# Gate and value written to HBM separately, and multiplied when the down projection loads them

## The chip, the cores and the metric

The kernel runs on one core of a Trainium2 chip. The metric is the device time of one execution in microseconds (us), lower is better. The engines are PE (matrix products; PEld is its weight load), DVE (vector), ACT (activation), POOL (GpSimd; here it mostly issues DMAs) and SP (it only issues DMAs). They run side by side, each in its own fixed order, and wait for one another by semaphores. The order on each engine is set when the kernel is built.

## What is computed

One decoder layer over 512 positions and 2048 channels: a token mixer of four parallel groups, an output projection, and a channel mixer. Only the channel mixer is touched:

```
def conv_ffn(h, up, conv_w, conv_b, down):
    hid = causal_dwconv(h @ up, conv_w, conv_b)      # 2 x 5632 channels, width 3
    gate, val = jnp.split(hid, 2, axis=-1)
    return (jax.nn.gelu(gate) * val) @ down          # 5632 -> 2048
```

All data are float32. A product of two float32 matrices is made of three products of split operands: each operand is a high part (rounded by a cast on ACT, L159 or L1047) and a low part (operand minus high part, a subtraction on DVE, L160 or L1048), and `mul3` (L207 to L211) adds high x high (L209), low x high and high x low (L210, L211).

## The kernel before

The 5632 hidden channels are 44 blocks of 128 channels x 512 positions; f counts them. For each f the **up phase** makes the gate block and the value block. For f from 3 to 43 `up_pair` (L1003) does this with seven smaller products instead of eight, in this order: p1 (B11), p5 (T1), p6 (T2), p2 (B21), p7 (T3), p4 (T4), p3 (B22), each of 24 matmuls over 256 columns. One pass over f is called a pair below; there are 41 of them.

Each pair loads four weight pieces of 512 KB through SP: r11, r21, r22, r12. They go round three buffers `raw`, so a load waits until DVE and ACT have read what the buffer held. DVE forms sums of them (`s1` = r21 + r22, then `s2`, and r21 + r11 in place) and the low parts (`wlo`), ACT the high parts (`whi`). r12 takes the buffer that r11 leaves; the r22 of the next pair takes the buffer that this pair's r22 leaves. Then `gated` (L935) runs the convolution on both blocks (ACT L327, then two steps of DVE L329 for each of gate `fcg` and value `fcv`), the gelu on ACT (L939), the product on DVE (L942), and POOL writes the block to HBM as `gd[f]` (L943).

The **down phase** loads the 44 blocks back, 22 in each half h. `load_g` (L1038) puts a block into a part of `act_hi`/`act_lo` that the up phase no longer reads, or into a buffer `gb`, and splits it. `GAT` (L1034) names the part: blocks 0 to 7 get parts that come free while the last pair runs, 12 to 15 those that its product p4 reads, 8 to 11 those that its p3 reads. PE then multiplies blocks and down weights into banks `pd`, 12 matmuls of 512 columns for one block. The weights are loaded by SP and split like those of the up phase; `whi` and `wlo` have four buffers each.

POOL issues its DMAs in one order: what stands behind a DMA that waits, waits too. The tiles with tag t (`fg`, `fv`, `fcg`, `fcv`, later the four rows of the post-norm) share eight buffers. The scheduler that sets the order simulates the program; so a change in one place can move instructions elsewhere.

Of the kernel before, what the change touches and what calls it, by code (L numbers as in the profile page):

```python
# [7 lines left out]
F32 = mybir.dt.float32  # L8
# [3 lines left out]
ALU = mybir.AluOpType  # L12
# [3 lines left out]
P = 128  # L16
S = 512
# [6 lines left out]
NF = DFF // P  # L24
# [32 lines left out]
def trunk(ctx: ExitStack, tc: tile.TileContext, x, xT, cols, rows, gdn_row, sgu_row, w_in, w_ba,  # L57
          lru_wa, lru_wx, sgu_ws, w_out, ffn_up, ffn_down, out):
    nc = tc.nc
    v, a, g, pe = nc.vector, nc.scalar, nc.gpsimd, nc.tensor  # L60
# [7 lines left out]
    dr = ctx.enter_context(tc.tile_pool(name="dr", bufs=1, space=DRAM))  # L68
# [9 lines left out]
    def new(tag, name, dt=F32):  # L78
        return tp.tile([P, S], dt, tag=tag, name=name, bufs=NBUF[tag])

    def T(name):
        return new("t", name)
# [34 lines left out]
    def col(name, i=0):  # L117
        o, _ = _OFF[name]
        return colt[:, o + i:o + i + 1]
# [141 lines left out]
    for c in range(DC):  # L261
        raw = []
# [58 lines left out]
    def conv(dst, src, taps, bias=None):  # L321

        n = len(taps)
        if bias is None:
            a.activation(out=dst, in_=src, func=AF.Copy, scale=taps[-1])
        else:
            a.activation(out=dst, in_=src, func=AF.Identity, scale=taps[-1], bias=bias)  # L327
        for j in range(1, n):
            v.scalar_tensor_tensor(out=dst[:, j:], in0=src[:, :S - j], scalar=taps[n - 1 - j], in1=dst[:, j:],  # L329
                                   op0=ALU.mult, op1=ALU.add)  # L330
# [62 lines left out]
    for t in range(NTT):  # L393
# [21 lines left out]
                    in1=gcum.rearrange("p t h -> p (t h)"), op=ALU.subtract)  # L415
# [407 lines left out]
    def B(name, dt=F32):  # L823
        return tp.tile([P, 2 * S], dt, tag="b", name=name, bufs=18)

    def side(t, i):
        return t[:, i * S:(i + 1) * S]
# [59 lines left out]
    for t in range(NTT):  # L887
# [22 lines left out]
        for d in range(DC):  # L910
# [3 lines left out]
            if d % 2 == 0:  # L914
# [4 lines left out]
                            in1=colt[:, o + 4 * d:o + 4 * d + 4].rearrange("p (k o) -> p k o", o=1)  # L919
# [2 lines left out]
            a.copy(out=hh, in_=blk(h1))  # L922
            v.tensor_tensor(out=hl, in0=blk(h1), in1=hh.bitcast(F32), op=ALU.subtract)  # L923

    gd = [dr.tile([P, S], F32, name=f"gd{f}") for f in range(NF)]
    o_cv = _OFF["ffn_conv"][0] + 3 * NF
    ncv = tp.tile([P, 3 * NF], F32, tag="ncv", name="ncv", bufs=1)
    v.tensor_scalar_mul(ncv, colt[:, o_cv:o_cv + 3 * NF], -1.0)
# [1 line left out]
    def taps(f, minus=False):  # L930
        if minus:
            return [ncv[:, 3 * (f - NF) + i:3 * (f - NF) + i + 1] for i in range(3)]
        return [col("ffn_conv", 3 * f + i) for i in range(3)]

    def gated(f, gs, vs, minus):  # L935

        gt = T("fcg")
        conv(gt, gs, taps(f), bias=col("ffn_cb", f))
        a.activation(out=gt, in_=gt, func=AF.Gelu_apprx_tanh)  # L939
        vt = T("fcv")  # L940
        conv(vt, vs, taps(NF + f, minus), bias=col("ffn_cb", NF + f))
        v.tensor_tensor(out=vt, in0=vt, in1=gt, op=ALU.mult)  # L942
        nc.gpsimd.dma_start(out=gd[f], in_=vt)  # L943

    NPL = 3
    for f in range(2):
        gemm_half(1, *first[f])
    gated(0, first[0][0], first[1][0], False)


# [20 lines left out]
    for f in range(1, NPL):  # L971
        pg, pv = (gemm_T(ffn_up, ff * P) for ff in (f, NF + f))
        gated(f, pg, pv, False)
# [29 lines left out]
    def up_pair(f):  # L1003
        r11, r21, r22, r12 = (load(ffn_up, k0, 8, ff * P, P) for ff, k0 in
                              ((f, 0), (NF + f, 0), (NF + f, 8), (f, 8)))
        s1, s2 = B("s1"), B("s2")
        gs, vs = T("fg"), T("fv")
        g1, g2, v1, v2 = gs[:, 0:H2], gs[:, H2:], vs[:, 0:H2], vs[:, H2:]
        add(s1, r21, r22)
        p1 = product(split(r11), "B11")  # L1010
        a.copy(out=v1, in_=p1)
        add(s2, s1, r11)
        p5 = product(split(s1), "T1")
        add(r21, r21, r11)
        p6 = product(split(s2), "T2")
        add(g2, v1, p6)
        p2 = product(split(r12), "B21")
        add(g1, v1, p2)
        add(s2, s2, r12)
        p7 = product(split(r21), "T3")  # L1020
        add(v1, g2, p7)
        add(v2, v1, p5)
        add(g2, g2, p5)
        p4 = product(split(r22), "T4")
        add(v1, v1, p4)
        p3 = product(split(s2), "B22")
        add(g2, g2, p3)
        gated(f, gs, vs, True)
# [9 lines left out]
    def load_g(f, i):  # L1038
        if i < 16:
            t, k = GAT[i]  # L1040
            hi, lo = (u[:, t, 4 * k:4 * k + 4, :].rearrange("p k c -> p (k c)") for u in (act_hi, act_lo))
        else:
            b = B("gb", F32R)
            hi, lo = side(b, 0), side(b, 1)
        raw = lo.bitcast(F32)
        nc.gpsimd.dma_start(out=raw, in_=gd[f])
        a.copy(out=hi, in_=raw)  # L1047
        v.tensor_tensor(out=lo, in0=raw, in1=hi.bitcast(F32), op=ALU.subtract)  # L1048
        return hi, lo

    fb = [[B("facc") for _ in range(2)] for _ in range(NTT)]
# [33 lines left out]
    for h in range(2):  # L1085
        gs = []
        for c in range(DC):
            banks = [bank("pd") for _ in range(NTT)]
            by_k = NH // 2 if h == 0 or c < DC - 1 else 7
            for i in range(by_k):  # L1090
                if c == 0:
                    gs += [load_g(h * NH + 2 * i + n, 2 * i + n) for n in range(2)]
                wt = weights(h, i, c)
                for n in range(2):
                    k = 2 * i + n
                    for t in range(NTT):
                        mul3(banks[t], cut(gs[k], TS[t]), wt[n], k == 0, k == NH - 1)
            if h == 1 and c == DC - 1:
                x1r = []
                for t in range(NTT):  # L1100
                    x1r.append((act_hi, act_lo)[t % 2][:, t // 2].rearrange("p k c -> p (k c)").bitcast(F32))
                    nc.sync.dma_start(out=x1r[t], in_=x1d[TS[t], :])
                wts = [weights(h, i, c) for i in range(by_k, NH // 2)]
            for t in range(NTT):
                if h == 1 and c == DC - 1:
                    for i, wt in enumerate(wts):
                        for n in range(2):
                            k = 2 * (by_k + i) + n
                            mul3(banks[t], cut(gs[k], TS[t]), wt[n], False, k == NH - 1)
                if h == 0:  # L1110
                    a.copy(out=facc[t][c], in_=banks[t])
                    continue
                v.tensor_tensor(out=facc[t][c], in0=banks[t], in1=facc[t][c], op=ALU.add)
                finish(t, c)
# [62 lines left out]
```

## Time and profile before

| | |
|---|---|
| time of three runs | 2188.92, 2192.87, 2194.44 us (median 2192.87) |
| the profiled execution | 2188.41 us, its span 2186.7 us |
| PE busy | 2150.3 us (98%), 13146 matmuls |
| DVE busy | 1389.4 us (64%) |
| ACT busy | 895.5 us (41%) |
| POOL busy | 133.5 us (6%) |
| up phase, pairs alone | about 855 to 1689 us from the span's start |
| down phase | about 1689 us to the end |
| gd written | 44 DMAs of 256 KB, median 4.4 us from issue to landing |
| gd loaded | 44 DMAs of 256 KB, medians 4.0 us (32 into act_lo) and 4.9 us (12 into gb) |

The busy share of an engine is an average; which wait ends last in a stage is what sets its time. A busy PE has matmuls that overlap (each is shown 0.28 us long, while they start every 0.12 us), so a short stall of PE is seen in the starts of its matmuls rather than as idle time.

### The profile page before, as it was taken

To read this page: it belongs to the slowest core of one execution; us is meant where nothing else is said; L and a number is where in the kernel's file an instruction comes from. 1 tells how busy PE (TensorE), PEld (TensorE's weight loads), DVE (VectorE), ACT (ScalarE), POOL (GpSimd) and SP (SyncE) were. 2 spreads that over 40 slices of the span, in tenths; PEclk is the share of its full clock that TensorE was granted. 3 is DMA by queue.
4 is the path that set the end of the run, shared out by engine and by line. 5 is a ranking of instruction groups with operands and counts; after the bars stand their busy time and mean duration, and the time that the engine had idled before them with its cause. 6 is when DMAs were issued, how large, how long until landed. Compare 5 with 4: busy or idle time off the path is not lost.

```text
span 2186.7 us, 32062 instructions
## 1 busy us (share of the span) xinstructions
PE 2150.3 (98%) x13146; PEld 1922.1 (88%) x13146; DVE 1389.4 (64%) x1869; ACT 895.5 (41%) x1255; POOL 133.5 (6%) x192
## 2 busy tenths in 40 slices
PE   8999999999999999999999999999999999999997
PEld 7788888888878888999999999999999888888885
DVE  6774454844552496888899999898889322423333
ACT  6564252522432473434444444444445312422222
POOL 0001010101100110000000000000002000100002
PEclk9999999999999999999999999999999999999998
DMA  9233222323232443334344434433436522532233
GB/s 299 68 88 87 68 78 78 78 77 87 87 123 102 155 131 103 115 111 120 105 124 121 119 115 124 122 116 112 122 116 206 179 97 97 166 114 97 96 114 147
DMA packets 316691, 254.85 MB, mean 117 GB/s; under 512 B 10496, under 2 KB 265216, under 8 KB 316032
## 3 DMA queue, kind: packets, MB, share of 16 engines
q1 hardware_dynamic: 304768, 219.24, 33.5%
q0 software_dynamic: 8320, 27.27, 3.4%
q10 hardware_dynamic: 3456, 6.29, 0.9%
q8 instruction: 103, 1.69, 0.3%
q14 instruction: 44, 0.36, 0.0%
HBM read 232.85 MB, written 19.92 MB: 116 GB/s over the span
## 4 chain that ended last, share of the span: by engine, by line
PE 72%; issue 14%; DVE 6%; DMA 6%; ACT 1%; POOL 1%; DVEq 0%; SPq 0%; ACTq 0%; POOLq 0%
PE pT L211 12%; PE pT L210 12%; PE pT L209 12%; DMA raw<-in_ffn_up_dram 5%; PE pd L209 4%; PE pB L211 4%; PE pd L210 4%; PE pB L210 4%; PE pB L209 4%; PE pd L211 4%; PE pwo L211 2%; PE pwo L209 2%; PE pwo L210 2%; DVE wlo L160 2%; DVE s L1001 1%
## 5 line engine op out<-in xcount | busy, mean ns | idle before, releaser
L160 DVE TENSOR_TENSOR wlo<-raw,whi 128x1024 fp32r<-128x1024 f32 x378 | 463.7, 1227 | 449.1 <-ACT whi L159 447.5
L159 ACT CAST whi<-raw 128x1024 fp32r<-128x1024 f32 x378 | 396.1, 1048 | 766.6 <-PE pd L211 295.3
L210 PE MATMUL pT<-act_lo,whi 128*128 128x512 f32 (+1 forms) x1032 | 365.0, 354 | 2.7 <-DVE act_lo L923 2.7
L209 PE MATMUL pT<-act_hi,whi 128*128 128x512 f32 (+1 forms) x1032 | 364.7, 354 | 0.4 <-ACT act_hi L922 0.4
L211 PE MATMUL pT<-act_hi,wlo 128*128 128x512 f32 (+1 forms) x1032 | 364.5, 353 | 0.0
L211 PE MATMUL pT<-eh,wlo 128*128 128x256 f32 x984 | 278.1, 283 | 5.0 <-DVE wlo L160 4.8
L211 PE MATMUL pB<-act_hi,wlo 128*128 128x256 f32 x984 | 278.9, 283 | 0.5 <-DVE wlo L160 0.3
L209 PE MATMUL pB<-act_hi,whi 128*128 128x256 f32 x984 | 278.4, 283 | 0.0
L210 PE MATMUL pB<-act_lo,whi 128*128 128x256 f32 x984 | 278.3, 283 | 0.0
L209 PE MATMUL pT<-eh,whi 128*128 128x256 f32 x984 | 277.1, 282 | 0.0
L210 PE MATMUL pT<-el,whi 128*128 128x256 f32 x984 | 277.0, 282 | 0.0
L159 ACT CAST whi<-s 128x1024 fp32r<-128x1024 f32 x123 | 128.5, 1044 | 231.6 <-DVE s L1001 176.6
L210 PEld LDWEIGHTS pT<-act_lo,whi 128*128 128x128 f32 x1032 | 195.9, 190 | 27.8 <-DVE act_lo L923 2.9
L211 PEld LDWEIGHTS pT<-act_hi,wlo 128*128 128x128 f32 x1032 | 196.0, 190 | 24.9 <-issue 1.0
L209 PEld LDWEIGHTS pT<-act_hi,whi 128*128 128x128 f32 x1032 | 195.8, 190 | 25.0 <-issue 0.7
L209 PE MATMUL pd<-whi,act_hi 128*128 128x512 f32 x512 | 198.5, 389 | 1.0 <-ACT whi L159 1.0
L211 PE MATMUL pd<-whi,act_lo 128*128 128x512 f32 x512 | 199.4, 389 | 0.0
L210 PE MATMUL pd<-wlo,act_hi 128*128 128x512 f32 x512 | 199.3, 389 | 0.0
L211 PEld LDWEIGHTS pT<-eh,wlo 128*128 128x128 f32 x984 | 185.2, 188 | 7.2 <-DVE wlo L160 7.2
L211 PEld LDWEIGHTS pB<-act_hi,wlo 128*128 128x128 f32 x984 | 188.6, 192 | 1.5 <-DVE wlo L160 1.5
L209 PEld LDWEIGHTS pB<-act_hi,whi 128*128 128x128 f32 x984 | 188.7, 192 | 0.2
L210 PEld LDWEIGHTS pB<-act_lo,whi 128*128 128x128 f32 x984 | 188.6, 192 | 0.0
(370 smaller groups left out, 3518.5 us busy)
## 6 DMA issues: line engine op xcount, KB each, us to landing
raw<-in_ffn_up_dram SPq DMA_DIRECT2D x176, 512.0 KB, 4.1
raw<-in_ffn_down_dram SPq DMA_DIRECT2D x88, 512.0 KB, 3.7
raw<-in_w_in_dram SPq DMA_DIRECT2D x86, 512.0 KB, 3.9
raw<-in_w_out_dram SPq DMA_DIRECT2D x32, 512.0 KB, 3.9
gd<-fcv POOLq DMA_DIRECT2D x44, 256.0 KB, 4.4
act_lo<-gd POOLq DMA_DIRECT2D x32, 256.0 KB, 4.0
xs<-in_xT_dram SPq DMA_DIRECT2D x16, 256.0 KB, 6.3
xn<-in_x_dram SPq DMA_DIRECT2D x16, 256.0 KB, 6.1
```

The lines of the kernel that those rows point to most:

```text
L159: a.copy(out=hi, in_=r)
L160: v.tensor_tensor(out=lo, in0=r, in1=hi.bitcast(F32), op=ALU.subtract)
L209: pe.matmul(p, lhsT=lt[0], rhs=rt[0], start=first, stop=False)
L210: pe.matmul(p, lhsT=lt[0], rhs=rt[1], start=False, stop=False)
L211: pe.matmul(p, lhsT=lt[1], rhs=rt[0], start=False, stop=last)
L1001: v.tensor_tensor(out=o, in0=x, in1=y, op=ALU.add)
```

## The change

The product on DVE (L942) goes out of `gated`. Gate and value are written to HBM as two blocks, `gd[f]` and `vd[f]`. In the down phase `load_g` loads both, the value into a new tile `vr` of tag t, multiplies them on DVE, and splits the product.

```
-    gd = [dr.tile([P, S], F32, name=f"gd{f}") for f in range(NF)]
+    gd, vd = ([dr.tile([P, S], F32, name=f"{n}{f}") for f in range(NF)] for n in ("gd", "vd"))
...
-        v.tensor_tensor(out=vt, in0=vt, in1=gt, op=ALU.mult)
-        nc.gpsimd.dma_start(out=gd[f], in_=vt)
+        nc.gpsimd.dma_start(out=gd[f], in_=gt)
+        nc.gpsimd.dma_start(out=vd[f], in_=vt)
...
         raw = lo.bitcast(F32)
         nc.gpsimd.dma_start(out=raw, in_=gd[f])
-        a.copy(out=hi, in_=raw)
-        v.tensor_tensor(out=lo, in0=raw, in1=hi.bitcast(F32), op=ALU.subtract)
+        vr = T("vr")
+        nc.gpsimd.dma_start(out=vr, in_=vd[f])
+        v.tensor_tensor(out=vr, in0=raw, in1=vr, op=ALU.mult)
+        a.copy(out=hi, in_=vr)
+        v.tensor_tensor(out=lo, in0=vr, in1=hi.bitcast(F32), op=ALU.subtract)
```

In the changed kernel the writes are L942 (gd) and L943 (vd), the load of the value L1048, the product L1049, the cast L1050 and the subtraction L1051. The instructions move at three places.

DVE at the start of the sixth pair (f = 8). `wlo<-raw` is the low part of r11, `s<-raw` is s1, `raw<-raw` frees r11. Before:

```order
L942 TENSOR_TENSOR fcv<-fcv,fcg 128x512
L1001 TENSOR_TENSOR fg<-fv,pT_7726 128x256
L160 TENSOR_TENSOR wlo<-s_7657,whi 128x1024
L1001 TENSOR_TENSOR fg<-fv,pB_7756 128x256
L1001 TENSOR_TENSOR s_7894<-raw 128x1024
L160 TENSOR_TENSOR wlo<-raw,whi 128x1024
L1001 TENSOR_TENSOR s_7895<-s_7894,raw 128x1024
L1001 TENSOR_TENSOR raw<-raw 128x1024
```

and now:

```order
L1001 TENSOR_TENSOR fg<-fv,pT_7770 128x256
L160 TENSOR_TENSOR wlo<-s_7701,whi 128x1024
L1001 TENSOR_TENSOR fg<-fv,pB_7800 128x256
L160 TENSOR_TENSOR wlo<-raw,whi 128x1024
L1001 TENSOR_TENSOR s_7938<-raw 128x1024
L1001 TENSOR_TENSOR fv<-fg,pT_7831 128x256
L1001 TENSOR_TENSOR s_7939<-s_7938,raw 128x1024
L1001 TENSOR_TENSOR raw<-raw 128x1024
```

The low part of r11 now stands ahead of s1. Before, it stands behind s1 in the first nine pairs and ahead of it from the tenth on; now it stands behind it in the first five only.

POOL at the end of the up phase, from the DMAs that wait for the last pair's p3 on. Before:

```order
L1046 DMA act_lo_91<-gd8_6233 128x512
L1046 DMA act_lo_91<-gd10_6235 128x512
L1046 DMA act_lo_91<-gd9_6234 128x512
L1046 DMA act_lo_91<-gd11_6236 128x512
L943 DMA gd42_6267<-fcv_16210 128x512
L943 DMA gd43_6268<-fcv_16448 128x512
```

and now:

```order
L1046 DMA act_lo_91<-gd9_6234 128x512
L1046 DMA act_lo_91<-gd11_6236 128x512
L1048 DMA vr_16513<-vd0_6269 128x512
L1048 DMA vr_16519<-vd1_6270 128x512
L1048 DMA vr_16555<-vd2_6271 128x512
L1048 DMA vr_16561<-vd3_6272 128x512
L1048 DMA vr_16597<-vd4_6273 128x512
L943 DMA vd43_6312<-fcv_16492 128x512
L942 DMA gd43_6268<-fcg_16487 128x512
L1048 DMA vr_16603<-vd5_6274 128x512
```

All value loads, that of block 0 first, stand behind the loads of blocks 9 and 11, which wait for the last up product.

ACT at the same place. `fcg` and `fcv` are the last pair's convolution, L939 its gelu, `whi` weights. Before:

```order
L1047 CAST act_hi<-act_lo 128x512 x3
L159 CAST whi<-raw 128x1024
L327 ACTIVATE fcg<-fg,colt 128x512
L327 ACTIVATE fcv<-fv,colt,ncv 128x512
L831 DMA row<-in_rows_dram 128x512 x4
L159 CAST whi<-raw 128x1024
L939 ACTIVATE fcg<-fcg 128x512
```

and now:

```order
L159 CAST whi<-raw 128x1024 x4
L327 ACTIVATE fcg<-fg,colt 128x512
L327 ACTIVATE fcv<-fv,colt,ncv 128x512
L939 ACTIVATE fcg<-fcg 128x512
L1050 CAST act_hi<-vr 128x512 x8
L159 CAST whi<-raw 128x1024
```

The last pair's convolution and gelu come ahead of the first cast of a loaded block, where they stood behind nearly all of them. On PE, the three down matmuls that stood inside the last pair's p3 now stand behind it.

## Rows read from the trace of the kernel before

**Rows 1.** Stretches: length, busy PE, PEld, DVE, ACT, POOL; granted clock, DMA share, GB/s.
```profile
860.00:1106.00 246.00, 241.66 (x2000) 239.26 (x2000) 211.07 (x266) 107.47 (x126) 6.27 (x12) 1.00 0.39 113
1106.00:1600.00 494.00, 494.00 (x4139) 493.99 (x4138) 450.10 (x569) 230.86 (x273) 13.49 (x25) 1.00 0.41 120
```
**Rows 2.** What PE waited for, whole span: us in total, times, longest us.
```profile
PE pT L211 <- DVE wlo L160: 4.8, 9, 0.7
PE pT L210 <- DVE act_lo L923: 2.7, 1, 2.7
PE pt L913 <- ACT xr L907: 2.3, 1, 2.3
```
**Rows 3.** PE in order of time: first matmul of T1 in two neighbouring pairs, twice.
```profile
1002.40 0.28 PE L209 MATMUL pT<-eh,whi 128*128 128x256 f32 x1
...
1023.54 0.28 PE L209 MATMUL pT<-eh,whi 128*128 128x256 f32 x1
...
1406.98 0.28 PE L209 MATMUL pT<-eh,whi 128*128 128x256 f32 x1
...
1427.04 0.28 PE L209 MATMUL pT<-eh,whi 128*128 128x256 f32 x1
```
**Rows 4.** DVE in order of time, s1 of the ninth pair: start, us, idle before.
```profile
1018.39 1.23 DVE L1001 TENSOR_TENSOR s<-raw 128x1024 f32<-128x1024 f32 x1 [2.96 <-DMA raw<-in_ffn_up_dram]
```
**Rows 5.** DVE in order of time, a late pair and the end of the up phase.
```profile
1657.05 0.74 DVE L329 SCALAR_TENSOR_TENSOR fcv<-fv,ncv,fcv 128x510 f32<-128x510 f32 x1
1657.71 1.22 DVE L160 TENSOR_TENSOR wlo<-raw,whi 128x1024 fp32r<-128x1024 f32 x1
...
1659.18 0.69 DVE L942 TENSOR_TENSOR fcv<-fcv,fcg 128x512 f32<-128x512 f32 x1
...
1664.31 1.22 DVE L1001 TENSOR_TENSOR s<-raw 128x1024 f32<-128x1024 f32 x1 [1.84 <-DMA raw<-in_ffn_up_dram]
...
1702.82 0.41 DVE L1001 TENSOR_TENSOR fg<-fg,pB 128x256 f32<-128x256 f32 x1
...
1707.48 0.74 DVE L329 SCALAR_TENSOR_TENSOR fcv<-fv,ncv,fcv 128x510 f32<-128x510 f32 x1
```
**Rows 6.** The chain that ended last, middle of the up phase: start, us, what.
```profile
1055.02 4.85 DMA raw<-in_ffn_up_dram
```
**Rows 7.** The same chain, last pairs of the up phase.
```profile
1647.72 3.84 DMA raw<-in_ffn_up_dram
...
1658.96 5.26 DMA raw<-in_ffn_up_dram
```
**Rows 8.** Weight tiles from 1106 to 1600 us: first and last start of s1.
```profile
L1001 DVE TENSOR_TENSOR s<-raw x24: 1224/1226/1227, 1120.4 to 1581.7; 128x1024 f32<-128x1024 f32 x24
```
**Rows 9.** POOL in order of time at the end of the up phase.
```profile
1660.16 0.54 POOL L943 DMA_DIRECT2D gd<-fcv  x1 [19.58 <-DVE fcv L942]
...
1689.44 1.09 POOL L1046 DMA_DIRECT2D act_lo<-gd  x2 [0.35 <-PE pB L211]
```
**Rows 10.** PE where the phases meet: first down matmuls, last up matmul.
```profile
1683.04 0.96 PE L209 MATMUL pd<-whi,act_hi 128*128 128x512 f32 x3 [0.96 <-ACT whi L159]
...
1688.98 0.28 PE L211 MATMUL pB<-act_hi,wlo 128*128 128x256 f32 x1
```
**Rows 11.** DMAs of gd: landing from 1686.7 to 1690.4 us, then whole run.
```profile
DMA to landing us min/median/max: 4.1/6.8/7.9
...
DMA to landing us min/median/max: 2.3/4.3/8.4
```
**Rows 12.** ACT: cast of a loaded block.
```profile
1690.99 0.62 ACT L1047 CAST act_hi<-act_lo 128x512 fp32r<-128x512 f32 x1 [1.31 <-DMA act_lo<-gd]
```
**Rows 13.** Stretches after PE's waits near 790 us, columns as in rows 1.
```profile
798.40:801.80 3.40, 2.98 (x14) 2.98 (x15) 3.40 (x6) 1.42 (x3) 0.00 (x0) 0.50 0.00 0
801.80:805.00 3.20, 3.20 (x28) 3.20 (x28) 3.20 (x6) 0.50 (x1) 0.00 (x0) 1.00 0.02 5
```
**Rows 14.** A stretch of the down phase, columns as in rows 1.
```profile
1900.00:2000.00 100.00, 100.00 (x438) 82.15 (x437) 33.00 (x35) 29.41 (x39) 4.16 (x8) 1.00 0.36 118
```

## The prediction
> **What bounds the kernel now.** I read the stretches of the span first, then what PE waited for, then DVE and the chain that ended last inside the up phase, and last the engines where the two phases meet.
>
> PE is busy nearly all the time. In the middle of the up phase it never idles, while DVE is busy 450 of 494 us [rows 1]. All that PE ever waits for is small; the largest entry is 4.8 us in nine waits for the low part of a weight [rows 2]. So work taken from DVE or ACT is worth what it does to a wait of PE, and no more.
>
> The up phase stands closer to a second limit than that table shows. One pair takes PE 20.06 us when nothing is late (1427.04 less 1406.98), but 21.14 us in the ninth pair (1023.54 less 1002.40) [rows 3]. The reason is a loop through DVE and SP. DVE frees the buffer of r22 with a `wlo`, SP loads the next r22 into it, and DVE waits for that load before s1: 2.96 us in the ninth pair, 1.84 us in a late one [rows 4, 5]. From s1 to the next release DVE works almost without a pause, and in that time r12 must land too. The middle 24 s1 start on average every (1581.7 - 1120.4)/23 = 20.06 us [rows 8]. That is just PE's own period: the loop has nothing to spare, and a later landing of r22 is paid by PE.
>
> The landing of r22 depends on what else moves. r12, with no write beside it, takes 3.84 us; r22, in whose time the write of `gd` falls, takes 4.85 and 5.26 us [rows 6, 7].
>
> In the down phase PE is never short of anything: 100 of 100 us busy, DVE 33, POOL 4 [rows 14]. Blocks are fetched well ahead.
>
> **The change part by part.** The sum is made against the profiled execution: 2188.41 us, span 2186.7. The median of the three runs is 4.46 us above it.
>
> *The product leaves the up phase.* 41 times 0.69 us of DVE in the pairs [rows 5]. It stands between the `wlo` that frees r22's buffer (ends 1658.93) and s1 (1664.31), and there DVE idles 1.84 us for the load anyway [rows 5]. Cover: that wait. I take 0. Bounds: 0, and a gain of the 4.8 us that PE waits for DVE in all [rows 2].
>
> *The order on DVE.* In four pairs, the sixth to the ninth, the low part of r11 moves from behind s1 into the wait ahead of it. That takes its 1.22 us (as the other `wlo` of that form [rows 5]) out of the loop. A pair of the old order costs 21.14 and one of the new 20.06 us [rows 3]: 4 x 1.08 = 4.3 us gained. Bounds: 0 and, with the pairs that follow late, 5.
>
> *The second write.* POOL now issues two DMAs for each pair. The value is ready when its second convolution step ends, 1657.05 + 0.74 = 1657.79; POOL starts 0.29 us after its releaser (L942 ends 1659.87, POOL 1660.16), so `vd` goes at 1658.08 and `gd`, 0.54 us later, at 1658.62 [rows 5, 9]. r22's load is issued at 1658.96 [rows 7]. Before, one write came 1.20 us after it and met its end; now two come 0.88 and 0.34 us ahead and meet its start. No row shows two. Lower bound 0: the first of them falls between the loads, and the other costs what one costs today. Upper bound: as much again as one costs, 4.85 - 3.84 = 1.0 us for each pair. I take 0.4, a little under the middle, since a good part of `vd` should have moved before r22's data start. From the sixth pair on that is 36 pairs x 0.4 = 14.4 us; range 0 to 36.
>
> The Trainium skill, "DMA: Bandwidth & Descriptors", section "Issuing engines are not separate DMA queues", says that DMAs started by SP, ACT and GpSimd all end on the same 16 engines and interleave, so the POOL queue shields the load from nothing. Rows 6 and 7 agree with it. Its fit for a DMA (section "Anatomy of one DMA") moves 256 KB in an estimated 0.6 us; at that price the term would be 36 x 0.6 = 21.6 us and the sum below 7 us higher.
>
> *Where the phases meet.* Before, all blocks were on their way while the last pair ran, and the first down matmuls started at 1683.04, after a wait of 0.96 us, inside the last pair [rows 10]. Now the value of block 0 stands behind the loads of blocks 9 and 11, which wait for the last up product. Count from that product's last matmul, at 1688.98 [rows 10]. POOL goes on 0.46 us later (1689.44) and needs 1.09 us for the two loads [rows 9], so `vr` of block 0 is issued at +1.55. Landings of such loads in this stretch have a median of 6.8 us; over the run the median is 4.3, the least 2.3, the largest 8.4 [rows 11]. I take 5.5, between the two medians: it lands at +7.05. Then come the product on DVE (0.69, as L942) and the cast on ACT (0.62) [rows 5, 12], and PE starts at +8.4. It would have gone on at +0.1, so the hole is 8.3, less the 0.96 that goes away: +7.3. Lower bound: the last convolution stands ahead of both on DVE and ACT; from its first sum to its end it takes 1702.82 to 1708.22, 5.4 us [rows 5], then 0.69 + 0.62 gives 6.7, so +5.6. Upper bound with 8.4 for the landing: 1.55 + 8.4 + 1.31 = 11.3, so +10.2. Behind the waiting `vr` loads stand the last two writes and the other values; behind the casts on ACT stands the fifth down weight. PE needs a block every 12 x 0.228 = 2.7 us (438 matmuls in 100 us [rows 14]), while POOL issues a load in 0.55 us and DVE spends two passes of 0.69 on a block, so from the second block on the supply keeps ahead.
>
> *The clock behind the hole.* Near 790 us PE waits 2.3 and 2.7 us [rows 2], and then the granted clock is 0.50, the 1.2 GHz level, for 3.4 us: 14 matmuls there, 28 in the next 3.2 us at 2.4 GHz [rows 13]. Fourteen matmuls at 3.2/28 = 0.114 us are 1.6 us lost. A hole of 8 us should do the same. I take 1.5; bounds 0 and 1.6. The Trainium skill, "TensorE: Matmul & The Clock Gate", section "Part 1: The HAM clock gate", says that a slow clock is the default and that activity lifts it, which rows 13 bear out; by that rule every long hole is paid twice, and this change makes one where there was none.
>
> *In the down phase.* 44 products of 0.69 us on DVE (30 us, where it is a third busy) and 44 loads of 0.55 us on POOL (24 us) [rows 5, 9, 14]. In the second half four buffers of tag t are left for `vr`; one turn is 5.5 + 0.69 + 0.62 + 0.69 = 7.5 us, for four blocks, against the 4 x 2.7 = 10.9 that PE takes for them. Hidden: 0. Without this cover the 22 products of a half would cost 15 us.
>
> Sum: -4.3 + 14.4 + 7.3 + 1.5 = +18.9, so 2207.3 against the profiled execution and, with the 4.5 us by which the median lies above it, 2211.8; I say 2211 us, 0.8% slower.
>
> **The rivals.**
>
> *The second write costs nothing.* Then the up phase gains its 4.3 us and the hole stays: -4.3 + 0 + 7.3 + 1.5 = +4.5, or +1.3 with the hole's lower bound and no slow clock. 2194 to 2197 us, no change. For it: r22's tail is then free of a write, and the load may land earlier than today's 4.85 to 5.26 us. It decides at a landing of r22 of about 4.7 us. Against it: two writes now stand ahead of r22 in the same transfer window. Chance 0.16.
>
> *The second write costs its full microsecond.* -4.3 + 36 + 8.8 = +40.5, so 2233 us. For it: rows 6 and 7 show one write at 1.0 to 1.4 us. Against it: half of the first write's time lies ahead of r22. Chance 0.15, taken from 2225 on.
>
> *The loads starve the second half.* POOL's order mixes gate loads, which wait for PE, with value loads, which wait for a buffer. If each block came 0.7 us late, 22 x 0.7 = 15 us on top: 2226 us. Against it: the turn of 7.5 us above. Chance 0.03.
>
> *Faster.* If PE's waits for the low parts all went (-4.8), the order gained 4.3 and the writes cost nothing, the hole at its least (5.6) would leave -3.5, still no change; for more, the first value would have to land before the last product ends, which the order on POOL excludes. Chance 0.04.
>
> **How the numbers follow.** Runs of this kernel spread by 0.3%, about 6.6 us; that is what a measurement can tell from no change. Forecast, +8 to +30: 0.62. Hidden write 0.16, all of it inside 0.3%. Full price 0.15 and starving 0.03, both slower. Faster 0.04. So slower 0.80, same 0.16, faster 0.04. The range runs from 2195, inside the hidden write's case, to 2232, close to the full price. The likeliest case alone is 2201 to 2223.
>
> **What would show it.** In the profile after: one hole of PE of 7 to 9 us between the last up matmul and the first down matmul, ended by a cast of `vr`, with a granted clock of 0.50 behind it; s1 waiting over 2 us for r22, with landings of r22 over 5 us; starts of T1 20.4 to 20.6 us apart from the eighth pair on, and 20.06 if the write is hidden; DVE with 28 us less before the hole and 30 more after it, without effect on PE. I am wrong if PE's starts in the up phase stay 20.06 us apart, if PE starts the down phase within 4 us, or if it waits in the second half.

## The result and the profile after

The changed kernel takes 2245.09 us (median of four runs, 2239.6 to 2247.0) against 2193.22 us for the kernel before (median of four, 2188.9 to 2194.4): ratio 1.0232, 95% interval 1.0215 to 1.0249. It is slower, as forecast, but by 52 us instead of 18. The profiled execution takes 2239.6 us, its span 2237.9 us, 51.2 us more than the span of before.

The stretches of the up phase (columns as in rows 1) and PE's waits (as in rows 2):

```profile
860.00:1106.00 246.00, 237.07 (x1968) 235.24 (x1967) 199.72 (x248) 105.55 (x124) 11.77 (x22) 1.00 0.43 124
1106.00:1600.00 494.00, 471.05 (x3896) 466.16 (x3894) 410.20 (x514) 215.52 (x255) 24.62 (x46) 1.00 0.43 124
```
```profile
PE pT L211 <- DVE wlo L160: 37.2, 37, 1.7
PE pd L209 <- ACT act_hi L1050: 15.0, 1, 15.0
```

In [rows 1] PE was busy in all 494 us of the middle; now 23 are missing. Its waits for a low part, 4.8 us in nine [rows 2], are 37.2 us in 37: nearly every pair. And one wait of 15.0 us is new.

The weight tiles of the middle (first and last s1, as in rows 8), one s1 on DVE (as in rows 4), and three steps of the chain of waits: a load of r12, then two of r22 (as in rows 6 and 7):

```profile
L1001 DVE TENSOR_TENSOR s<-raw x24: 1224/1226/1227, 1104.9 to 1594.4; 128x1024 f32<-128x1024 f32 x24
```
```profile
1104.90 1.23 DVE L1001 TENSOR_TENSOR s<-raw 128x1024 f32<-128x1024 f32 x1 [2.93 <-DMA raw<-in_ffn_up_dram]
```
```profile
1087.69 3.98 DMA raw<-in_ffn_up_dram
1099.06 5.75 DMA raw<-in_ffn_up_dram
...
1120.16 6.19 DMA raw<-in_ffn_up_dram
```

A pair now takes (1594.4 - 1104.9)/23 = 21.28 us; it took 20.06 [rows 8]. r22 lands after 5.75 and 6.19 us; r12, with no write beside it, still takes 4 us. From the first T1 to the last, 40 pairs apart, are 848.0 us (857.40 to 1705.39), where they were 811.5 (857.92 to 1669.41): **36.5 us of the 51 are lost here**.

POOL beside that load of 1099.06 (vd, then gd):

```profile
1098.42 0.54 POOL L943 DMA_DIRECT2D vd<-fcv  x1 [20.68 <-ACT fcg L939]
1098.95 0.54 POOL L942 DMA_DIRECT2D gd<-fcg  x1
```

They go 0.64 and 0.11 us ahead of r22, where the prediction had put them at 0.88 and 0.34.

Where the phases meet: PE's last up and first down matmul; POOL from the writes of the last pair but one to the first value load; the chain there; the stretches of the hole and behind it, and one of the down phase.

```profile
1724.28 0.28 PE L211 MATMUL pB<-act_hi,wlo 128*128 128x256 f32 x1
1739.60 0.79 PE L209 MATMUL pd<-whi,act_hi 128*128 128x512 f32 x1 [15.04 <-ACT act_hi L1050]
```
```profile
1716.67 0.55 POOL L943 DMA_DIRECT2D vd<-fcv  x1 [5.84 <-ACT fcg L939]
...
1717.74 0.55 POOL L1046 DMA_DIRECT2D act_lo<-gd  x1
1720.68 3.78 POOL L1046 DMA_DIRECT2D act_lo<-gd  x7 [2.39 <-issue]
1725.59 0.55 POOL L1046 DMA_DIRECT2D act_lo<-gd  x1 [1.13 <-DMA act_lo<-gd]
1726.98 0.55 POOL L1046 DMA_DIRECT2D act_lo<-gd  x1 [0.84 <-DMA act_lo<-gd]
1728.23 0.55 POOL L1046 DMA_DIRECT2D act_lo<-gd  x1 [0.71 <-DMA act_lo<-gd]
1729.10 0.55 POOL L1046 DMA_DIRECT2D act_lo<-gd  x1 [0.32 <-DMA act_lo<-gd]
1730.20 0.55 POOL L1048 DMA_DIRECT2D vr<-vd  x1 [0.56 <-DMA act_lo<-gd]
```
```profile
1721.77 7.04 DMA act_lo<-gd
1730.20 7.91 DMA vr<-vd
```
```profile
1724.50:1739.60 15.10, 0.06 (x1) 0.00 (x0) 6.66 (x9) 4.50 (x6) 6.55 (x12) 0.67 1.02 387
1739.60:1743.40 3.80, 3.80 (x9) 3.03 (x10) 3.80 (x8) 2.45 (x4) 2.10 (x4) 0.51 0.65 236
1743.40:1747.20 3.80, 3.80 (x18) 3.13 (x18) 3.80 (x7) 1.96 (x5) 1.71 (x4) 1.00 0.97 318
1900.00:2000.00 100.00, 100.00 (x439) 82.19 (x438) 49.62 (x62) 36.59 (x49) 19.60 (x36) 1.00 0.58 190
```

The hole is 15.04 us, where 8.3 were forecast. The value of block 0 is issued 5.92 us behind the last up matmul and needs 7.91 us to land. The four block loads ahead of it and the value itself each start 0.28 to 0.52 us after the landing of the eighth DMA before them on POOL: the load of 1721.77 lands at 1728.81, and the eighth behind it starts at 1729.10. In the whole trace no DMA of POOL starts sooner than 0.28 us after that landing. In the hole the 16 DMA engines are busy all the time (share 1.02, 387 GB/s): it is a stretch of transfers, with PE waiting. Behind it the granted clock is 0.51, the level of 1.2 GHz, and PE starts 9 matmuls in 3.8 us, 18 in the next 3.8: 1.9 us lost. Later in the down phase PE is busy 100 of 100 us, as in [rows 14].

Sum: 36.5 + (15.04 - 0.96) + 1.9 = 52.5. The last down matmul comes 53.0 us later (2223.77 less 2170.76). The span grew by 51.2 only, because the stretch from that matmul to the end took 14.1 us instead of 15.9; over all kernels here it varies from 10.5 to 16.0, so single runs are compared by stages below.

### The profile page after: what moved, and what is told of

Its sections match the earlier page's. It is cut to its first block, busy times and chain, and to the rows that moved or that the text cites. A ratio compares the mean times of both kernels' runs of the same rounds, so it can differ in the third digit from the quotient of the medians.

```text
span 2237.9 us, 32269 instructions
## 1 busy us (share of the span) xinstructions
PE 2157.2 (96%) x13146; PEld 1925.0 (86%) x13146; DVE 1390.0 (62%) x1869; ACT 895.9 (40%) x1255; POOL 180.4 (8%) x280
## 3 DMA queue, kind: packets, MB, share of 16 engines
q0 software_dynamic: 15360, 50.34, 6.6%
## 4 chain that ended last, share of the span: by engine, by line
PE 42%; issue 25%; DMA 16%; DVE 14%; POOL 2%; ACT 1%; DVEq 0%; SPq 0%; POOLq 0%; ACTq 0%
DMA raw<-in_ffn_up_dram 15%; PE pT L211 8%; PE pT L210 8%; PE pT L209 8%; DVE s L1001 3%; DVE wlo L160 3%; PE pwo L211 3%; PE pwo L209 2%; PE pwo L210 2%; DVE fcv L329 2%; DVE fcg L329 2%; DVE raw L1001 1%; ACT whi L159 1%; POOL vr L1048 1%; DVE fv L1001 1%
## 5 line engine op out<-in xcount | busy, mean ns | idle before, releaser
L211 PE MATMUL pT<-eh,wlo 128*128 128x256 f32 x984 | 281.1, 286 | 37.2 <-DVE wlo L160 37.2
```

The source lines that it names most:

```text
L211: pe.matmul(p, lhsT=lt[1], rhs=rt[0], start=False, stop=last)
```

## Experiments

The theory after the result: **L**, the writes hold up r22, and the loop through DVE and SP hands that on to PE; **H**, the hole is the first value loads, issued late and landing late. "r22" below is the mean landing of 40 loads that s1 waits for, "T1" the time from the first T1 to the last.

**E1, two writes early, one load.**
```
-        vr = T("vr") ... a.copy(out=hi, in_=vr)      # load_g of the changed kernel
+        a.copy(out=hi, in_=raw)                       # load_g of before: gd alone
```


> Gate and value are both written in the up phase as in the change, but the down phase loads and splits the gate block alone (the product is left out). Theory (the second write delays r22, and the loop through DVE and SP passes that on to PE): first to last T1 takes about 848 us as in the change (811.5 in the kernel before), r22 lands about 5.9 us after its issue, and the hole between the phases is back to about 1 us; 2188 + 36 = about 2225 us. Rival (the loss in the up phase comes from something else, such as buffers of tag t held by the value loads): T1 back to about 811 us and about 2190 us in all.


Measured: 2225.54 us, T1 849.8 us, r22 5.99 us; PE goes from the last up matmul to a down matmul in 0.12 us. The up phase's loss needs nothing of the down phase.

```profile
PE pT L211 <- DVE wlo L160: 38.8, 36, 2.2
```

**E2, two writes late.**
```
         v.tensor_tensor(out=vt, in0=vt, in1=gt, op=ALU.mult)
         nc.gpsimd.dma_start(out=gd[f], in_=vt)
+        nc.gpsimd.dma_start(out=vd[f], in_=vt)
```


> The kernel before, with the product written twice, to gd and to vd; both writes wait for the product, so they are issued about 1.2 and 1.7 us after the load of r22 instead of ahead of it. Volume theory (each 256 KB that moves while r22 moves costs it): r22 lands after about 5.9 us, first to last T1 about 848 us, about 2225 us in all. Position theory (what costs is that writes are issued at the start of r22, not that there are two): r22 at 4.8 to 5.2 us, T1 811 to 822 us, 2188 to 2200 us.


Measured: 2186.70 us, T1 814.0, r22 4.92 us. The same bytes as in the changed kernel, 1.8 us later, cost 2.5 us instead of 36. The plain volume theory falls.

```profile
PE pT L211 <- DVE wlo L160: 6.8, 12, 1.0
```

**E3, one write early.**
```
-        v.tensor_tensor(out=vt, in0=vt, in1=gt, op=ALU.mult)
         nc.gpsimd.dma_start(out=gd[f], in_=vt)
```


> The kernel before with the product left out and the value block alone written (the gelu isn't used): one write for each pair, issued about 0.1 to 0.7 us ahead of the load of r22, with the DVE order of the changed kernel. Volume theory: r22 lands after 4.5 to 4.9 us, T1 at 805 to 812 us (the better order on DVE shows its 4 us), 2182 to 2190 us. Position theory: r22 about 5.9 us, T1 about 848 us, about 2225 us.


Measured: 2192.72 us, T1 812.0, r22 4.98 us. One write at the early place costs about as much as the one write of the kernel before (T1 811.5), so the place alone isn't it. DVE stands in the order of the changed kernel here: the sixth to tenth T1 intervals sum to 101.4 us, against 105.7 in the kernel before. The difference is the 4.3 us that the prediction gave to that order, but the write moved as well, so the run does not show that the order alone made it. It is lost again later, where pairs of 20.06 us have become pairs of up to 20.7.

**E5, two writes early with half the bytes.**
```
-        nc.gpsimd.dma_start(out=gd[f], in_=gt)
-        nc.gpsimd.dma_start(out=vd[f], in_=vt)
+        nc.gpsimd.dma_start(out=gd[f][:, 0:H2], in_=gt[:, 0:H2])
+        nc.gpsimd.dma_start(out=gd[f][:, H2:], in_=vt[:, H2:])
```


> As the run with gate and value both written early, but each write carries half of its block (128 KB), both into one block that the down phase loads (half of the gate and half of the value; the product is left out). Two writes at the same places, with the bytes of one. Theory (what delays r22 is the bytes that move inside its landing time, about 1.0 us for 256 KB): r22 lands after about 5.0 us as with one early write, T1 from first to last 811 to 822 us. Rival (each write costs its microsecond by being there, whatever its size): r22 about 5.9 us, T1 about 848 us.


Measured: 2194.37 us, T1 818.3, r22 5.11 us. It is mostly the bytes at that place and not the number of writes: two halves cost T1 6.3 us more than one whole write (E3), two whole writes 36.0 more. DVE has the order of the kernel before in this run, so not all of the 6.3 need be the second write's.

**E9 and E10, the writes from ACT's and from SP's queue.**
```
-        nc.gpsimd.dma_start(out=gd[f], in_=gt)
-        nc.gpsimd.dma_start(out=vd[f], in_=vt)
+        nc.scalar.dma_start(out=gd[f], in_=gt)       # E10: nc.sync
+        nc.scalar.dma_start(out=vd[f], in_=vt)
```


> The changed kernel, with both writes issued by ACT (its own DMA queue) instead of POOL, behind the gelu and a cast. Theory (what counts is the bytes that move inside r22's landing, whichever engine issues them): r22 lands after about 5.9 us, T1 from first to last about 848 us; POOL no longer waits for the gelu of the pair before the last, so the act_lo loads go out with the products and the first value load at about +1.7 to +5 us behind the last up matmul instead of +5.9; hole 11 to 15 us. Rival (the queue of POOL is what slows r22): r22 under 5.3 us and T1 below 830 us.

> The changed kernel, with both writes issued by SP, in the same queue as the loads and ahead of r22's. Theory (bytes inside the landing): r22 is issued two DMA issues later or moves with both writes, and s1 starts at least as late as in the changed kernel, T1 from first to last 848 us or more. Rival (the queue of POOL is what slows r22; a queue that works in order lets the writes go out ahead of the load): T1 below 830 us.


Measured: 2221.19 and 2223.54 us, T1 827.4 and 827.6, r22 5.43 and 5.40 us, holes of 12.3 and 14.5 us from matmul to matmul. The rivals' T1, below 830 us, came true in both, r22 under 5.3 us did not, and the theory's 848 us did not either: of the 36.5 us some 16 stay with another queue, some 20 go. The DMA issues by kind (KB each, median us to landing), of the changed kernel and of E9:

```profile
gd<-fcg POOLq DMA_DIRECT2D x44, 256.0 KB, 5.5
vd<-fcv POOLq DMA_DIRECT2D x44, 256.0 KB, 4.4
```
```profile
gd<-fcg ACTq DMA_DIRECT2D x44, 256.0 KB, 4.4
vd<-fcv ACTq DMA_DIRECT2D x44, 256.0 KB, 3.7
```

From ACT they are issued some 0.5 us earlier (1.08 and 0.71 us ahead of r22) and land faster, gd 3.8 us after r22's issue instead of 5.5. So less of them is left when r22's last bytes move. The packets differ too. The queues with their packets, MB and share, of the changed kernel and of E9 (the weights are in q1):

```profile
q1 hardware_dynamic: 304768, 219.24, 33.0%
q0 software_dynamic: 15360, 50.34, 6.6%
```
```profile
q10 hardware_dynamic: 16128, 29.37, 4.1%
```

A packet of POOL's queue carries 50.34 MB/15360 = 3.3 KB on average, one of ACT's 29.37/16128 = 1.8 KB, one of the weights 0.7 KB. The Trainium skill, "DMA: Bandwidth & Descriptors", section "Queues, rings and completion order", says that an engine takes turns between its queues packet by packet; by that rule larger packets take a larger share from the weights, if the profile's packets are the ones it means. No run here varies the packets alone. How much is this and how much the earlier issue, these runs do not part.

**E11, no write at all.**
```
-        v.tensor_tensor(out=vt, in0=vt, in1=gt, op=ALU.mult)
-        nc.gpsimd.dma_start(out=gd[f], in_=vt)
+        if f == 0:
+            nc.gpsimd.dma_start(out=gd[f], in_=vt)
...
-        nc.gpsimd.dma_start(out=raw, in_=gd[f])
+        nc.gpsimd.dma_start(out=raw, in_=gd[0])
```


> The kernel before without the writes of the up phase: only block 0 is written (its value), and the down phase loads that block 44 times; the product is left out. Theory (about 1.0 us of r22's landing for each 256 KB that moves in it): r22 lands after 3.9 to 4.1 us, so that 0, 256 and 512 KB give 4.0, 5.0 and 5.9 us, and T1 starts 20.06 us apart but for the early pairs, 802 to 806 us from first to last. Rival (part of r22's landing is its own, since it follows r21 by 2.5 us): r22 stays at 4.6 us or more and T1 near 810 us.


Measured: 2180.66 us, T1 802.4 (40 x 20.06), r22 4.56 us. The time is the theory's, the landing nearly the rival's: r22 has 4.56 us of its own, so the first 256 KB cost 0.3 to 0.4 us and not the 1.0 that the prediction read from r12. DVE has the order of the kernel before here, and still every pair takes 20.06 us: that order costs nothing where r22 is early enough.

| writes of a pair, issue against r22's | r22 us | T1 us | PE waits for wlo us |
|---|---|---|---|
| none (E11) | 4.56 | 802.4 | 0.3 |
| 256 KB, +1.2 (before) | 4.85 | 811.5 | 4.8 |
| 512 KB, +1.2 and +1.7 (E2) | 4.92 | 814.0 | 6.8 |
| 256 KB, -0.6 (E3) | 4.98 | 812.0 | 5.4 |
| 2 x 128 KB, -0.6 and -0.1 (E5) | 5.11 | 818.3 | 10.8 |
| 512 KB, -1.1 and -0.7, ACT (E9) | 5.43 | 827.4 | 16.5 |
| 512 KB, -0.6 and -0.1 (after) | 5.92 | 848.0 | 37.2 |

T1 follows r22. The late rows fit a threshold of some 4.75 us, beyond which each microsecond of landing costs a pair about one (after: 848.0/40 = 21.2 us, and 20.06 + 5.92 - 4.75 = 21.23; E9: 20.7 and 20.74). Close to it the mean says less: before pays 0.23 us a pair at 4.85.

**E4, the loop taken away: r22 in another buffer, in the changed kernel.**
```
-        r11, r21, r22, r12 = (load(ffn_up, k0, 8, ff * P, P) for ff, k0 in
-                              ((f, 0), (NF + f, 0), (NF + f, 8), (f, 8)))
+        r11, r21, r22, r12 = (load(ffn_up, k0, 8, ff * P, P, raw=B("r22") if i == 2 else None)
+                              for i, (ff, k0) in
+                              enumerate(((f, 0), (NF + f, 0), (NF + f, 8), (f, 8))))
```


> The changed kernel, with r22 loaded into a buffer of tag b (18 of them, some free during the up phase) instead of the three buffers raw, so that its load no longer waits for this pair's r22 to be read. Loop theory: the load comes early enough to hide its landing, T1 starts 20.06 us apart, 802 to 812 us from first to last, the hole of 15 us stays: 2245 - 36 to 46 = about 2200 to 2209 us. Rival (DMA engines or DVE themselves cannot keep up): T1 stays above 830 us and the time above 2225 us.


Measured: 2189.97 us, T1 802.4 with every pair at 20.06 us, r22 4.16 us. L is borne out: both writes are there, the DMAs move 132 GB/s, and PE idles in none of the 494 us of the middle. The run takes away two things at once: r22 no longer waits for its buffer, and so it goes out 3.1 us ahead of vd and lands about when vd's data begin to move.

```profile
1106.00:1600.00 494.00, 494.00 (x4139) 494.00 (x4138) 445.93 (x545) 239.85 (x270) 25.80 (x48) 1.00 0.45 132
...
1678.80:1689.50 10.70, 0.06 (x1) 0.00 (x0) 5.21 (x8) 3.69 (x5) 5.45 (x10) 0.74 1.04 388
```

The hole is shorter too, which I had not expected: 10.97 us from matmul to matmul, where the changed kernel has 15.32. POOL:

```profile
1679.04 1.09 POOL L1048 DMA_DIRECT2D act_lo<-gd  x2 [0.35 <-PE pB L212]
1680.12 1.08 POOL L1050 DMA_DIRECT2D vr<-vd  x2
```

The last up matmul starts at 1678.58, so the first value is issued at +1.54, the 1.55 of the prediction; it lands at 1688.06, after 7.94 us, and product and cast take 1.5. In the changed kernel issue is at +5.92, landing 7.91. So the difference is the issue alone: there the gelu of the last pair but one starts 9.0 us ahead of the last up matmul, in E4 15.5 us ahead. POOL waits 5.84 us for it at its write and then has twelve loads to catch up on, the last four of which, like the value, stand until the eighth DMA before them has landed.

**E6, the first four values loaded early, in the changed kernel.**
```
     for f in range(NPL, NF):
+        if f == NF - 1:      # vd[0] to vd[3] into two B tiles; load_g uses them
+            for j in range(2):
+                vb = B("vb")
+                for n in range(2):
+                    vre[2 * j + n] = side(vb, n)
+                    nc.gpsimd.dma_start(out=side(vb, n), in_=vd[2 * j + n])
         up_pair(f)
```


> The changed kernel, with the values of blocks 0 to 3 loaded ahead of the last pair's DMAs, into two buffers of tag b. Theory (the hole is the late issue and long landing of the first value loads): PE starts the down phase at the end of the last up product or before it, works 4 x 2.7 = 11 us on the four blocks, and then waits 3 to 6 us for block 4, whose value is now the first that POOL issues behind the last act_lo loads; the hole of 15 us falls to 3 to 6 us in all, last down matmul 9 to 13 us earlier counted from the last up matmul. Rival (the last pair's convolution and gelu, ahead on DVE and ACT, hold the first cast): the hole stays at 8 us or more.


Measured: 2238.91 us. PE goes on 0.12 us after the last up matmul, works 11 us on the four blocks and then waits 6.1 us for the fifth: H holds for the start, and the rival (convolution and gelu in the way) falls there. From last up to last down matmul 7.9 us are gained (491.6 instead of 499.5), less than the 9 to 13 expected, and the last T1 interval grew to 24.2 us, since two of the loads into gb now fall beside its r22 (8.58 us to landing). So the total gains little or nothing. PE's wait, and the DMAs while PE works on the four blocks and in the wait:

```profile
1748.79 0.79 PE L209 MATMUL pd<-whi,act_hi 128*128 128x512 f32 x1 [6.14 <-ACT act_hi L1059]
```
```profile
1731.50:1742.50 11.00, 11.00 (x50) 8.90 (x49) 6.14 (x11) 4.29 (x5) 4.17 (x8) 1.00 1.04 392
1742.50:1748.80 6.30, 0.15 (x2) 0.02 (x1) 4.04 (x6) 2.48 (x5) 2.17 (x4) 0.92 0.91 333
```

The value of block 4 is there at 1743.02, but its product stands on DVE behind two low parts of down weights, and those weights landed after 10.2 and 11.3 us. The DMA engines are full; what is not late as a value is late as a weight.

**E7, the same buffer for r22 in the kernel before.** The edit of E4, whose other half is in `load`:
```
-    def load(w, k0, nk, c0, nc_, pieces=1):
-        raw = wp.tile([P, 1024], F32, tag="raw", name="raw", bufs=3)
+    def load(w, k0, nk, c0, nc_, pieces=1, raw=None):
+        if raw is None:
+            raw = wp.tile([P, 1024], F32, tag="raw", name="raw", bufs=3)
```

> The kernel before, with r22 in a buffer of tag b, so that the loop through DVE and SP is gone. Loop theory: all pairs at 20.06 us as in the changed kernel with that buffer, 802.4 us from first to last T1 instead of 811.5, ratio to before 0.995 to 0.997. Rival (something else of the write costs PE time): ratio 0.999 to 1.001.


Measured: 2178.42 us, ratio 0.9937 (0.9920 to 0.9954), T1 802.4; somewhat better than expected. The loop cost the kernel before 9 us too.

```profile
860.00:1106.00 246.00, 246.00 (x2063) 246.00 (x2062) 225.34 (x279) 119.25 (x136) 6.47 (x12) 1.00 0.42 120
```

**E8, both mends in the changed kernel,** E4 and E6 together; in `load_g`:
```
-        vr = T("vr")
-        nc.gpsimd.dma_start(out=vr, in_=vd[f])
+        vr = vre.get(f)
+        if vr is None:
+            vr = T("vr")
+            nc.gpsimd.dma_start(out=vr, in_=vd[f])
```

> The changed kernel with both mends: r22 in a buffer of tag b, and the values of blocks 0 to 3 loaded ahead of the last pair's DMAs. Theory (the loop and the first value loads are all that the change costs): T1 802 us, hole 0 to 2 us, no clock drop behind it, ratio to the kernel before 0.993 to 0.998. Rival (a cost of the second write or of the value loads that is left in the down phase): ratio 1.000 or more.


Measured: 2179.29 us, ratio 0.9943 (0.9928 to 0.9958), T1 802.4, one wait of 1.7 us for the fifth block. Stretch of the last up matmul to the fifth block:

```profile
1678.80:1689.50 10.70, 10.70 (x48) 8.63 (x46) 5.48 (x7) 4.00 (x5) 5.45 (x10) 1.00 0.99 372
```

The same bytes move as in the hole of E4 (372 against 388 GB/s), but PE has four blocks to work on. The two mends take away all that the change cost; it then equals E7 within the intervals. Both are 0.6% faster than the kernel before, a small gain, but with intervals that stay below 1.

## Why the prediction was wrong

*Direction and places were right:* the loop through DVE and SP, the value loads behind the last act_lo loads, the slow clock behind the hole, nothing in the rest of the down phase. Two sizes were not, and the gain from the order on DVE did not show.

*The second write* was taken at 0.4 us of landing for each pair, 14.4 us in all, with 36 as the upper bound. It measured 5.92 - 4.85 = 1.07 us (0.94 against the one early write of E3), and the up phase came out at +36.5 instead of +10.1. The reason given for the low value was that "a good part of `vd` should have moved before r22's data start". That is what happened; the step that failed is the price put on it. These are the DMA queues of the changed kernel (packets, MB, share; q0 has POOL's writes, q1 the weights) from r22's issue at 1099.06 to 1100.60, then to 1102.50, 1103.90 and 1105.00:

```profile
q0 software_dynamic: 65, 0.24, 56.3%
q1 hardware_dynamic: 453, 0.22, 49.4%
...
q1 hardware_dynamic: 768, 0.39, 81.0%
q0 software_dynamic: 15, 0.02, 4.5%
...
q0 software_dynamic: 79, 0.26, 46.0%
q1 hardware_dynamic: 223, 0.11, 25.8%
...
q1 hardware_dynamic: 27, 0.01, 3.9%
```

And those of the kernel before, from the issue at 1055.02 [rows 6] to 1056.25, then to 1057.80 and 1059.50:

```profile
q1 hardware_dynamic: 498, 0.25, 67.5%
...
q1 hardware_dynamic: 673, 0.34, 81.5%
...
q1 hardware_dynamic: 351, 0.17, 34.6%
q0 software_dynamic: 71, 0.23, 33.8%
```

r22 is 0.52 MB, the last that q1 moves here. So its data begin at about 1100.60, when 0.24 of vd's 0.26 MB have moved: 1.5 us behind its issue, where it is 1.2 in the kernel before. vd ahead of r22 is not free, it makes r22 start later. And gd, taken to "meet its start", moves from 1102.50 on, 3.5 us behind its own issue, into the last quarter of r22; the single write of before met the last third. So vd's price comes on top of a write at r22's end that is still there. In this pair the later start is 0.3 of the 0.9 us (5.75 less 4.85). The other 0.6 fall between r22's first data and its landing, and what makes them is open.

So the rival "full microsecond" was right in the up phase; its objection, that half of the first write's time lies ahead of r22, saved nothing. Its price was right by accident: it took r12's 3.84 us for an r22 without a write, while that is 4.56 us (E11). The first write costs 0.3 us and the second 1.07, not 1.0 each.

The Trainium skill, "DMA: Bandwidth & Descriptors", section "Anatomy of one DMA", gave an estimated 0.6 us for 256 KB, 21.6 us in all; the rows give 1.07 us a pair, and 36.5 us for the up phase. Its section "Issuing engines are not separate DMA queues", by which the DMAs of all engines run on the same 16 DMA engines and interleave, is half borne out: moving the writes to ACT or SP leaves a loss of 16 us, but takes 20 us away.

*The order on DVE:* -4.3 us, from 21.14 less 20.06 us a pair. In the changed kernel the loop binds nearly every pair, and no gain is seen: from the sixth pair on the intervals are 20.7 us or more. The 1.08 us were not the order's alone: E11 has the old order and takes 20.06 us, while r22 in the fourth to tenth pairs of the kernel before lands after 5.1 to 5.4 us. The old order costs only together with such landings; E3 is consistent with a gain of 4.3 us, but no run changes the order alone.

*Where the phases meet:* +7.3 forecast, +14.1 measured. The landing was taken as 5.5 us, between the median of that stretch, 6.8, and that of the run [rows 11]; it is 7.91, because the value loads come on top in a stretch whose DMA engines were busy already. Before, while the last pair ran (columns as in rows 1):

```profile
1675.00:1690.00 15.00, 14.04 (x110) 13.45 (x109) 15.00 (x23) 13.84 (x22) 5.98 (x12) 1.00 0.84 267
```

At a share of 0.84 the stretch's own median was the nearer row. The issue was taken at +1.55 and is +5.92; E4 shows 1.54 where the up phase is not late. So 2.4 us are the landing, 4.4 the issue, and the latter is a second bill for the second write: I worked out the two terms apart, and they are coupled through POOL's order, in which the writes of the last pair but one now stand ahead of twelve loads. E9 bears this out: its gelu is as late (9.1 us ahead of the last up matmul), but POOL has no write to wait at, and the value is issued at +2.73.

*The clock:* 1.5 forecast, 1.9 measured. *The down phase:* 0, as forecast; DVE is busy 49.6 instead of 33 of 100 us there, and PE 100. *The product out of the up phase:* 0, as forecast; DVE has less to do (410 instead of 450 us) and waits longer.

*The threshold* of the first rival, a landing of 4.7 us, was close to the 4.75 that fits the table. With it the nearest check was at hand: before, the mean is already 4.85, so most of what comes on top is paid by PE (36.5/40 = 0.91 of 1.07 us).

## What to carry to other kernels

Where a loop of load, use and release has no slack, ask of each new transfer which load's landing its bytes fall into, from its first data to its last; 1.8 us later the same two writes were almost free, and one more buffer made them free altogether. Two DMAs side by side can cost more than twice one: the second write cost 0.94 to 1.07 us, the first 0.3 to 0.4. At a seam between phases count the bytes that have to pass it: when the DMA engines are full there, an earlier load only moves the wait, unless the engine has enough work in hand to cover the stretch.

## What the hardware showed that I had not expected

A write of 256 KB beside a load of 512 KB costs the load 0.3 to 0.4 us; a second one, both early, 0.4 us more from the queues of ACT or SP and 0.9 more from POOL's. With all 16 DMA engines busy (387 to 392 GB/s) loads of 256 KB took 7 to 9 us to land and weights of 512 KB up to 11.3, against 4 us for either in quieter stretches. A single hole of 15 us of PE was followed by 3.7 us at half the clock, hardly longer than the 3.4 us behind holes of 2 to 3 us in the kernel before [rows 13]. The second of two writes that POOL issued 0.5 us apart began to move its data only 3.5 us after its issue, the first after 1.1; and POOL never had more than eight DMAs that had not landed.
